# First projection unit among the indexer products, with loads fetched ahead and other homes for five kept units

## The chip, the cores and the metric

The kernel runs on one core of one Trainium2 chip. The metric is the device time of one execution in microseconds. Before the change three runs gave 2064.09, 2066.74 and 2067.27 us; the median is 2066.74 us. Times inside an execution come from one profiled execution, counted from its first instruction.

## The reference, cut to what matters

One layer of a streaming encoder, for 2048 tokens of width 1024, all in float32:

```
xn     = rms_norm(x, norm_gain)
proj   = xn @ w_in          # qa ka va ga | qb kb vb gb | iq ik iw | za zb
ya     = chunked_relpos_attention(qa, ka, va, rel_bias) * silu(ga)
iq, ik = partial_rope(iq), partial_rope(ik)
score  = sum over heads of relu(iq_h . ik) * iw_h      # chunk-causal
idx    = top 256 keys of each query by score
yb     = attention(qb over kb[idx], vb[idx]) * silu(gb)
merged = sigmoid(za + b_a) * (ya @ w_branch_a) + sigmoid(zb + b_b) * (yb @ w_branch_b)
out    = rms_norm(x + merged @ w_out, final_gain)
```

The change touches the projection of x, the loads around it, and where some intermediate results are kept. It changes no product.

## The kernel before, in words

**Precision.** Every float32 product is made from split operands: each operand is a rounded high part and a low part (the rest), and `mm3` (L213) issues three matmuls for each 128-row slice of the contraction: high x high, high x low, low x high. A product over the full width of 1024 and 512 tokens is 8 x 3 = 24 matmuls of 512 columns.

**First phase (L237 to L421), the index projection.** The tokens are four groups of 512. The phase takes them in the order 2, 3, 0, 1, so index i = 0 to 3 stands for groups 2, 3, 0, 1. For each index i there are three products, `chain(i, m)` with m = 0, 1, 2: rotated index queries and keys and part of kb; further index queries; the rest. x of a group lives in one of two slots (groups 2 and 0 in slot 0, groups 3 and 1 in slot 1). For i = 0 and 1 x is used before the norm (`split_u`), and the reciprocal root is multiplied in when the result leaves the accumulator. For i = 2 and 3 it is scaled first (`scaled`, through `split_x`, L231: a VectorE multiply L233, a ScalarE cast L234, a VectorE subtraction L235). The roots come from `squares` (row sums of squares, L287), `root_columns` (VectorE, L297) and `root_rows` (four transposes on TensorE, L307, and a ScalarE copy, L308). The rows of x for the squares are loaded by `load_rows` into tiles of other tags, "xr" and "e" among them. `evac_i` (L321) empties an accumulator: for m = 0 it loads a rotation table "cs" (L328, one buffer) and rotates; then it casts (L340), subtracts (L341) and stores to memory (L347). `weights_t` (L353) transposes the index weights. The seven accumulators of the chains are taken in turn by `rot("first", 7)`: acc0 and acc1 (pool psp), acc2 to acc4 (pool psx), "lg0" and "ptr0" (pool psl).

**Projection units.** The other columns of w_in are 20 units of 256 columns (`UNITS`, L67; unit 0 is the first of zb). `prep(u)` (L192) loads a unit's weights (L207), casts them on ScalarE (L209) and takes the low part on GpSimd (L210), into one of the two "wt" tiles; before the change the first of these uses a staging of two tiles of 128 KB. The two "wt" tiles hold x of index 0 and 2 and the index weights w01 during the first phase. The main loop (L1354) runs a list of jobs; a "std" job is one unit on group 0 or 1, two products of 24 matmuls each (L1373), emptied by `evac` (L688; zb takes a sigmoid with the bias table "bm", L700, and a store, L701). After job 0 the loop prepares unit 1, after job 1 unit 2.

**Half products.** For 18 of the units (`quads`) groups 2 and 3 are made with one product fewer, from sums and differences of x blocks and of weight blocks. A first turn (`first_half`, and `last_half` for the last unit) leaves three partial sums; a last turn (`part`, L1429) adds them in. Partial sums go to memory (`qD`) and come back (`load_sum`), except those of the units in `KEPT`, which stay on chip in tiles lent by `homes` (L1311). `turns` (L1399) sets the order of the last turns. From `last_half` to `part(0, 0)` TensorE's order is written by hand (`held`, a manual schedule). There `combine_pe` (L1247) makes differences of x blocks on TensorE with two unit matrices that `signs` keeps in a tile of tag "xs".

**Logits and search.** Index logits, scores and the threshold search of each block of 128 queries are written as two generators (`logits`, `search`). Every product of the main loop calls `tick`, which lets `pump` (L645) take steps of the two, as many as a budget of 4300 per tick allows by written costs. When both have ended, `search_again` (L578) writes a check: a flag is computed (L585 to L587), VectorE and GpSimd load it (L588) and branch (L589, L590) over a spare arm, `bits_of` (L595), which repeats the search in another way and is normally not run. Attention begins once tick 142 is passed.

**Order.** Except in that hand-written stretch, a planner orders the instructions of each engine at build time, from its own simulated times and the order in the text, with the text's order as priority. All loads and stores in question are issued from SyncE's one queue (SP).

Of the kernel before, what the change touches and what calls it, by code (L numbers as in the profile page):

```python
# [96 lines left out]
def block_kernel(ctx: ExitStack, tc: tile.TileContext, io, dbg=None):  # L97
# [93 lines left out]

    def prep(u, gate=None, at=None):  # L192
        if (at or u) in wcur:
            return
        wt = wpool.tile([128, 2, KT, WT], F32R, name="wt", tag="wt")
        if UNITS[u][0] == "va":
            st = stage[-1][0].tile([128, KT, 32], F32, name="wst", tag="wst", bufs=stage[-1][2])
            nc.sync.dma_start(st, io["wV"][UNITS[u][1]])
            nc.scalar.activation(wt[:, 0, :, 256:288], st, AF.Copy)
            nc.gpsimd.tensor_tensor(wt[:, 1, :, 256:288], st, f32(wt[:, 0, :, 256:288]), op=OP.subtract)  # L200
        for c in range(2):
            pl, n, bufs = stage[-1]
            for k in range(0, KT, n):
                st = pl.tile([128, n, 128], F32, name="wst", tag="wst", bufs=bufs)
                if gate is not None:
                    nc.gpsimd.tensor_copy(st[:, 0, 0:1], gate)
                nc.sync.dma_start(st, io["wP"][u, c, :, k:k + n, :])  # L207
                hi = wt[:, 0, k:k + n, c * 128:(c + 1) * 128]
                nc.scalar.activation(hi, st, AF.Copy)  # L209
                nc.gpsimd.tensor_tensor(wt[:, 1, k:k + n, c * 128:(c + 1) * 128], st, f32(hi), op=OP.subtract)  # L210
        wcur[at or u] = wt
# [19 lines left out]
    def split_x(s, k, src, root):  # L231

        nc.vector.scalar_tensor_tensor(src, src, gcol[:, k:k + 1], root, op0=OP.mult, op1=OP.mult)  # L233
        nc.scalar.activation(xh[s][:, k], src, AF.Copy)  # L234
        nc.vector.tensor_tensor(xl[s][:, k], src, f32(xh[s][:, k]), op=OP.subtract)  # L235

    with ExitStack() as ph:  # L237
# [74 lines left out]
        def chain(i, m, c=all_):  # L312
# [6 lines left out]
            mm3(accs[i, m][:, c], [((w_[0][:, k], w_[1][:, k]), (xh[s_][:, k, c], xl[s_][:, k, c])) for k in range(KT)])  # L319

        def evac_i(i, m):  # L321
            g = order[i]
# [3 lines left out]
            if m == 0:  # L326
                cs = xp.tile([128, 2, 512], F32, name="cs", tag="cs")
                nc.sync.dma_start(cs, io["csI"][:, :, cols])  # L328
                if i < 2:
# [29 lines left out]

        nc.sync.dma_start(gcol, io["g1"])  # L360
        for k in range(0, KT, 2):
            load_x(0, k, k + 2, halves[0])
# [34 lines left out]
        for m in range(3):  # L397
            chain(1, m)
        scaled(2)
        for m in range(3):  # L400
            evac_i(0, m)
        weights_t(0)
        for m in range(3):
            chain(2, m)
        squares(3)
        roots_of(3)
        squares(1)
        roots_of(1)
        scaled(3)
        prep(0)  # L410
        for m in range(3):
            evac_i(1, m)
        weights_t(1)
        for m in range(3):
            evac_i(2, m)
        for m in range(3):
            chain(3, m)
        weights_t(2)
        for m in range(3):
            evac_i(3, m)  # L420
        weights_t(3)  # L421


# [28 lines left out]
    ready, scores, open_ = [], {}, set()  # L452

    iqs = {}

    def load_iq(b):

        iqs[b] = tk.tile([128, H, 128], F32R, name="iqT", tag="iqT", bufs=2)
        for a in range(4):
            nc.sync.dma_start(f32(iqs[b][a * 32:a * 32 + 32]),  # L460
                              iqD[a % 2].rearrange("(d h) n -> d h n", h=H)[:, :, b * 128:b * 128 + 128])

    load_iq(BLOCKS[0])

# [130 lines left out]
    def bits_of(b):  # L595
# [6 lines left out]
        half = sc.bitcast(I16).rearrange("p (n t) -> p n t", t=2)  # L602
        hi, lo, eq = (q.tile([128, S], I16, name="i16" + t, tag=t)[:, :n]
                      for q, t in ((tk, "sc1"), (tkl, "sc2"), (tkl, "sc3")))
        junk = tk.tile([128, S], I16, name="junk16", tag="gt", bufs=2)[:, :n]
# [32 lines left out]

    nc.sync.dma_start(bm, io["bm"])
    threads = {0: logits(), 1: search()}  # L640
# [547 lines left out]
    def tick(x):  # L1188
        due[1] += x
        if threads:  # L1190
            pump(PUMP * x)
# [116 lines left out]

    KEPT, on_chip, free_ = quads[-6:], {}, []

    def homes(n):  # L1311

        while len(free_) < n:
            opened = count_["home"] = count_.get("home", -1) + 1
            if opened < 6:
                assert 0 not in threads
            else:
                assert not threads
            pl, tag, w, bufs = ((xpoolr, "ikT", S, 1), (tk, "iqT", 1024, 2), (tk, "iqT", 1024, 2), (xpoolr, "roots2", 512, 1),
                                (xpoolr, "roots3", 512, 1), (tkl, "xs", 1024, 2),  # L1320
                                (tk, "gt", 1024, 2), (tk, "gt", 1024, 2), (tk, "sc0", SLOTS[0], 1))[opened]
            t = pl.tile([128, w], F32R, name="keep" + tag, tag=tag, bufs=bufs)
# [31 lines left out]
    for i, (how, r_, u, g) in enumerate(jobs):  # L1354
        kind, c2 = UNITS[u]
        wt, s_ = wcur[r_], SLOT[g]
        if how == "one":
            for _ in (last_half if u == quads[-1] else first_half)(u, wt):
                tick(0.5)
        for c in range(0 if how == "one" else 4 if kind == "va" else 2):  # L1360
            acc = next_acc(i)
            if kind == "va":
# [35 lines left out]
    kept_ = list(KEPT)  # L1398
    turns = [(kept_ if q in (0, 1, 3, 5, 7, 9) else plain).pop(0) for q in range(len(quads))]  # L1399

# [210 lines left out]
```

## Time and profile before

| what | us |
| --- | --- |
| median of three runs | 2066.74 |
| profiled execution | 2061.87 |
| its span, first to last instruction | 2060.1 |
| TensorE busy | 1988.3 |
| VectorE busy | 1472.6 |
| ScalarE busy | 1261.9 |
| GpSimd busy | 801.6 |

Engines: PE is TensorE, PEld its weight loads, DVE VectorE, ACT ScalarE, POOL GpSimd, SP SyncE, whose queue issues the transfers. In the timeline a row gives start, length, engine, line, operation, written and read tile, partitions x elements, count; square brackets give the idle time just before it and what ended that. A letter q behind an engine (DVEq) marks work of its sequencer. A matmul's length overlaps the next one's; rates are counts over windows.

### The profile page before, as it was taken

To read this page: it belongs to the slowest core of one execution; us is meant where nothing else is said; L and a number is where in the kernel's file an instruction comes from. 1 tells how busy PE (TensorE), PEld (TensorE's weight loads), DVE (VectorE), ACT (ScalarE), POOL (GpSimd) and SP (SyncE) were. 2 spreads that over 40 slices of the span, in tenths; PEclk is the share of its full clock that TensorE was granted. 3 is DMA by queue.
4 is the path that set the end of the run, shared out by engine and by line. 5 is a ranking of instruction groups with operands and counts; after the bars stand their busy time and mean duration, and the time that the engine had idled before them with its cause. 6 is when DMAs were issued, how large, how long until landed. Compare 5 with 4: busy or idle time off the path is not lost.

```text
span 2060.1 us, 33967 instructions
## 1 busy us (share of the span) xinstructions
PE 1988.3 (97%) x10674; PEld 1690.0 (82%) x10674; DVE 1472.6 (71%) x3646; ACT 1261.9 (61%) x2481; POOL 801.6 (39%) x1045
## 2 busy tenths in 40 slices
PE   8799999999999999999979999999999999999998
PEld 7588888889889888778858889888888888887886
DVE  6749887978789987476446768758886688775534
ACT  5456666556567554247468869858987688773221
POOL 2122233321132464465335464454444633432410
PEclk9899999999999999999979999999999999999999
DMA  9473344374464665378797674564355631325632
GB/s 351 149 241 125 120 139 159 132 208 138 169 196 139 219 219 172 112 235 284 263 275 226 200 231 144 168 222 145 122 155 168 219 103 52 104 88 183 216 136 92
DMA packets 243144, 361.57 MB, mean 176 GB/s; under 512 B 30992, under 2 KB 114320, under 8 KB 242832
## 3 DMA queue, kind: packets, MB, share of 16 engines
q1 hardware_dynamic: 242960, 359.37, 54.3%
q8 instruction: 85, 1.39, 0.3%
q14 instruction: 99, 0.81, 0.1%
HBM read 243.45 MB, written 115.83 MB: 174 GB/s over the span
## 4 chain that ended last, share of the span: by engine, by line
PE 49%; DVE 3%; DMA 3%; ACT 2%; issue 2%; POOL 1%; SPq 0%; DVEq 0%; ACTq 0%; POOLq 0%
PE d L219 9%; PE po L1506 8%; PE acc L219 7%; PE O L1025 6%; PE s L1000 6%; PE pt L1017 5%; PE O L935 3%; PE s L890 3%; PE pt L925 3%; DMA wst<-wS 1%; DVE P L816 1%; DMA kk<-kA 1%; DVE ptl L840 0%; ACT P L1003 0%; DMA kBt<-kB 0%
## 5 line engine op out<-in xcount | busy, mean ns | idle before, releaser
L219 PE MATMUL acc<-xh,wt 128*128 128x512 f32 x2160 | 690.4, 394 | 6.8 <-DVE e L341 2.4
L219 PEld LDWEIGHTS acc<-xh,wt 128*128 128x128 f32 x2160 | 405.1, 188 | 99.1 <-ACT wt L1261 5.0
L219 PE MATMUL acc<-xl,wt 128*128 128x512 f32 x1080 | 423.6, 392 | 0.0
L837 POOL TENSOR_TENSOR ptl<-pf,pth 128x512 fp32r<-128x512 f32 (+1 forms) x144 | 179.9, 1249 | 256.7 <-ACT pf L833 179.5
L219 PEld LDWEIGHTS acc<-xl,wt 128*128 128x128 f32 x1080 | 203.7, 189 | 43.8
L210 POOL TENSOR_TENSOR wt<-wst,wt 128x512 fp32r<-128x512 f32 (+1 forms) x92 | 117.6, 1304 | 269.0 <-ACT wt L209 237.5
L840 DVE TENSOR_TENSOR ptl<-pt,pth 128x512 fp32r<-128x512 f32 (+1 forms) x288 | 187.5, 660 | 45.3 <-ACT pth L839 43.7
L490 DVE SCALAR_TENSOR_TENSOR sc<-lg,iw,sc 128x512 f32<-128x512 f32 (+2 forms) x266 | 178.9, 679 | 42.6 <-ACT lg L485 37.4
L1000 PE MATMUL s<-kBt,qsB 128*128 128x512 f32 (+3 forms) x640 | 187.3, 385 | 2.7 <-DVE mx L816 2.3
L485 ACT ACTIVATE lg<-lg 128x512 f32<-128x512 f32 (+2 forms) x304 | 149.8, 524 | 65.4 <-PE lg L483 63.8
L839 ACT ACTIVATE pth<-pt 128x512 fp32r<-128x512 f32 (+1 forms) x288 | 159.8, 579 | 30.4 <-PE pt L1017 19.9
L1017 PE MATMUL pt<-ident,P 128*128 128x128 f32 x1088 | 166.5, 273 | 1.1 <-DVE ptl L840 0.6
L1003 ACT ACTIVATE P<-P,mx 128x128 f32<-128x128 f32 (+15 forms) x128 | 154.7, 1210 | 18.6 <-DVE mx L816 18.3
L1025 PE MATMUL O<-ptl,vBt 128*128 128x256 f32 x544 | 149.0, 299 | 2.6 <-POOL ptl L837 1.8
L1025 PE MATMUL O<-pth,vBt 128*128 128x256 f32 x544 | 147.6, 289 | 2.5 <-ACT pth L839 1.0
L816 DVE CUSTOM_DVE_ANT_0 P<-s,mk,mx 128x512 f32<-128x512 f32 (+2 forms) x192 | 125.1, 651 | 33.7 <-PE s L1000 27.4
L1017 PEld LDWEIGHTS pt<-ident,P 128*128 128x128 f32 x1088 | 127.5, 140 | 9.2 <-DVE ptl L840 1.8
L890 PE MATMUL s<-kk,qz 128*128 128x320 f32 (+1 forms) x448 | 112.2, 348 | 12.3 <-DMA kk<-kA 8.9
L1064 POOL TENSOR_TENSOR dw<-dst,dw 128x512 fp32r<-128x512 f32 x64 | 83.0, 1298 | 82.3 <-ACT dw L1063 77.9
L1000 PEld LDWEIGHTS s<-kBt,qsB 128*128 128x128 f32 x640 | 102.0, 190 | 15.6 <-DVE mx L816 9.3
L1025 PEld LDWEIGHTS O<-ptl,vBt 128*128 128x128 f32 x544 | 102.6, 189 | 14.0 <-DVE ptl L840 6.7
L1261 ACT ACTIVATE wt<-wst 128x512 fp32r<-128x512 f32 (+1 forms) x144 | 72.9, 567 | 64.1 <-PE acc L219 36.6
(310 smaller groups left out, 4438.2 us busy)
## 6 DMA issues: line engine op xcount, KB each, us to landing
wst<-wP SPq DMA_DIRECT2D x84, 256.0 KB
wst<-wS SPq DMA_DIRECT2D x72, 256.0 KB
kk<-kA SPq DMA_DIRECT2D x56, 256.0 KB
vs<-vA SPq DMA_DIRECT2D x56, 256.0 KB
wst<-wS SPq DMA_DIRECT2D x72, 192.0 KB
qz<-qA SPq DMA_DIRECT2D x96, 128.0 KB
qD<-q SPq DMA_DIRECT2D x36, 256.0 KB
part<-qD SPq DMA_DIRECT2D x36, 256.0 KB
```

What stands on the lines that cost most here:

```text
L219: m = nc.tensor.matmul(acc, a, b, start=(first and i == 0), stop=(last and i == n - 1), **({} if first and last else {"skip_group_check": ...
L485: nc.scalar.activation(lg, lg, AF.Relu)
L490: nc.vector.scalar_tensor_tensor(o_, lg, wv, o_, op0=OP.mult, op1=OP.add)
L837: nc.gpsimd.tensor_tensor(lo, pf, f32(hi), op=OP.subtract)
L839: nc.scalar.activation(hi, src, AF.Copy)
L840: nc.vector.tensor_tensor(lo, src, f32(hi), op=OP.subtract)
L890: nc.tensor.matmul(s_ps[:, :w], q[:, m, j * 128:(j + 1) * 128], kk[:, ko:ko + w], start=(m == 0), stop=(m == 1))
L1000: nc.tensor.matmul(s_ps[:, :w], q[:, h, :], kBt[:, m, a:a + w], start=(m == 0), stop=(m == 1))
L1003: nc.scalar.activation(P[:, e, :n], P[:, e, :n], AF.Exp, bias=mx[:, e:e + 1], scale=-1.0, accum_out=st["sum"][:, (u % 2) * 2 + e:(u % 2) * ...
L1017: nc.tensor.transpose(pt[:, k, e, :], P[:, e, (kt + k) * 128:(kt + k + 1) * 128], ident)
L1025: nc.tensor.matmul(o_, vBt[:, kt + k, :], src[:, k, :], start=(kt + k == 0 and n_ == 0), stop=(kt + k == b and n_ == 1), skip_group_check= ...
L1506: nc.tensor.matmul(accs[t, hf], a, b[:, n_], start=(k == 0 and i == 0), stop=(k == KT - 1 and i == 2))
```

## The change

- Unit 0 on group 0 (job 0 of the main loop) is written in the first phase, after chain(2, ·) and the scaling of index 3. Its accumulators are acc2 and ptr0, and its two results leave with the sigmoid there. The main loop only counts job 0's two ticks.
- Unit 0's weights are prepared after `scaled(2)`, through the six small staging tiles "wis" of the index weights. Unit 1's are prepared the same way before the last `evac_i`.
- chain(2, ·) runs in the order m = 1, 0, 2; chain(2, 1) is emptied early. The root of index 3 is taken before that of index 1 and its transposes stand before chain(2, 2).
- The rotation tables of index 2 and 3 are loaded ahead into "xr" tiles. The first queries of the logits (`load_iq`) are loaded inside the phase. The bias table bm is loaded second, behind the gains.
- For the first four ticks `tick` does not pump.
- Five units are kept on chip instead of six. Their homes are ikT, two iqT, the two roots, sc2 and sc3; the spare arm takes sc1 and the two "xs" tiles. The order of the last turns follows.

```diff
-    def prep(u, gate=None, at=None):
+    def prep(u, gate=None, at=None, via=None):
...
-            pl, n, bufs = stage[-1]
+            pl, n, bufs = via or stage[-1]
             for k in range(0, KT, n):
-                st = pl.tile([128, n, 128], F32, name="wst", tag="wst", bufs=bufs)
+                st = pl.tile([128, n, 128], F32, name="wst", tag="wis" if via else "wst", bufs=bufs)
...
+        turns_ = {}
+
+        def load_cs(i, tag, bufs):
+            cs = xp.tile([128, 2, 512], F32, name="cs", tag=tag, bufs=bufs)
+            nc.sync.dma_start(cs, io["csI"][:, :, order[i] * 512:order[i] * 512 + 512])
+            return cs
...
-                cs = xp.tile([128, 2, 512], F32, name="cs", tag="cs")
-                nc.sync.dma_start(cs, io["csI"][:, :, cols])
+                cs = turns_.pop(i) if i in turns_ else load_cs(i, "cs", 1)
...
         nc.sync.dma_start(gcol, io["g1"])
+        nc.sync.dma_start(bm, io["bm"])
...
         scaled(2)
+        prep(0, via=(xp, 2, 6))
         for m in range(3):
             evac_i(0, m)
         weights_t(0)
-        for m in range(3):
-            chain(2, m)
         squares(3)
-        roots_of(3)
+        root_columns(3, 1)
+        chain(2, 1)
+        chain(2, 0)
+        root_rows(3)
+        chain(2, 2)
+        evac_i(2, 1)
+        scaled(3)
+        for c in range(2):
+            acc = (ps, psl)[c].tile([128, 512], F32, name="xa", tag=("acc2", "ptr0")[c])
+            c_ = slice(c * 128, c * 128 + 128)
+            mm3(acc, [((wcur[0][:, 0, k, c_], wcur[0][:, 1, k, c_]), (xh[0][:, k], xl[0][:, k])) for k in range(KT)])
+            e = ev.tile([128, 512], F32, name="ef", tag="ef")
+            nc.scalar.activation(e, acc, AF.Sigmoid, bias=bm[:, 8 + c:9 + c])
+            nc.sync.dma_start(sBD[0][c_], e)
+        rot("first", 7)
         squares(1)
+        for i in (2, 3):
+            turns_[i] = load_cs(i, "xr", 2)
         roots_of(1)
-        scaled(3)
-        prep(0)
         for m in range(3):
             evac_i(1, m)
         weights_t(1)
-        for m in range(3):
+        for m in (0, 2):
             evac_i(2, m)
         for m in range(3):
             chain(3, m)
         weights_t(2)
+        load_iq(BLOCKS[0])
+        prep(1, via=(xp, 2, 6))
         for m in range(3):
             evac_i(3, m)
...
-        hi, lo, eq = (q.tile([128, S], I16, name="i16" + t, tag=t)[:, :n]
-                      for q, t in ((tk, "sc1"), (tkl, "sc2"), (tkl, "sc3")))
+        hi, lo, eq = (q.tile([128, S], I16, name="i16" + t, tag=t, bufs=n_)[:, :n]
+                      for q, t, n_ in ((tk, "sc1", 1), (tkl, "xs", 2), (tkl, "xs", 2)))
...
-    nc.sync.dma_start(bm, io["bm"])
...
     def tick(x):
         due[1] += x
+        if due[1] <= 4:
+            return
...
-    KEPT, on_chip, free_ = quads[-6:], {}, []
+    KEPT, on_chip, free_ = quads[-5:], {}, []
...
             opened = count_["home"] = count_.get("home", -1) + 1
-            if opened < 6:
-                assert 0 not in threads
-            else:
-                assert not threads
+            assert 0 not in threads and open_ <= set(pairs[-1])
             pl, tag, w, bufs = ((xpoolr, "ikT", S, 1), (tk, "iqT", 1024, 2), (tk, "iqT", 1024, 2), (xpoolr, "roots2", 512, 1),
-                                (xpoolr, "roots3", 512, 1), (tkl, "xs", 1024, 2),
-                                (tk, "gt", 1024, 2), (tk, "gt", 1024, 2), (tk, "sc0", SLOTS[0], 1))[opened]
+                                (xpoolr, "roots3", 512, 1), (tkl, "sc2", SLOTS[2], 1),
+                                (tkl, "sc3", SLOTS[3], 1))[opened]
...
         for c in range(0 if how == "one" else 4 if kind == "va" else 2):
+            if i == 0:
+                tick(1)
+                continue
             acc = next_acc(i)
...
-    turns = [(kept_ if q in (0, 1, 3, 5, 7, 9) else plain).pop(0) for q in range(len(quads))]
+    turns = [(kept_ if q in (0, 1, 3, 5, 7) else plain).pop(0) for q in range(len(quads))]
```

`load_iq` moves up in the text, unchanged, so that the first phase can call it.

More of the change, by code (lines that the diff above doesn't have):

```diff
@@ L235, in split_x, with load_iq @@
         nc.vector.tensor_tensor(xl[s][:, k], src, f32(xh[s][:, k]), op=OP.subtract)
+    iqs = {}
+    def load_iq(b):
+        iqs[b] = tk.tile([128, H, 128], F32R, name="iqT", tag="iqT", bufs=2)
+        for a in range(4):
+            nc.sync.dma_start(f32(iqs[b][a * 32:a * 32 + 32]),
+                              iqD[a % 2].rearrange("(d h) n -> d h n", h=H)[:, :, b * 128:b * 128 + 128])
     with ExitStack() as ph:
@@ L452, in block_kernel @@
     ready, scores, open_ = [], {}, set()
[L454 to L463, printed above, removed]
     def logits():
```

## The prediction

> **What bounds the kernel now.** I read the page first, then the windows table of the opening 125 us, then TensorE's own timeline there, and only then the places that the later edits touch. The page:
>
> ```profile
> span 2060.1 us, 33967 instructions
> PE 1988.3 (97%) x10674; PEld 1690.0 (82%) x10674; DVE 1472.6 (71%) x3646; ACT 1261.9 (61%) x2481; POOL 801.6 (39%) x1045
> PE   8799999999999999999979999999999999999998
> PEclk9899999999999999999979999999999999999999
> ```
>
> TensorE is the bound: 1988.3 of 2060.1 us. An edit that removes no matmul can only win where TensorE stands still or runs below full clock; slices 1, 2 and 21 are such places. The change removes no matmul. The windows table (columns: window, length, busy time and count of each engine, granted clock, DMA share, GB/s), the last three rows of it finer:
>
> ```profile
> 0.00:25.00 25.00, 17.87 (x133) 17.83 (x134) 13.90 (x29) 17.29 (x38) 9.78 (x109) 1.00 0.86 294
> 25.00:50.00 25.00, 23.98 (x112) 19.54 (x112) 15.95 (x42) 12.41 (x25) 0.33 (x1) 1.00 1.03 405
> 50.00:75.00 25.00, 14.72 (x67) 10.93 (x65) 19.09 (x47) 15.37 (x32) 11.00 (x10) 0.89 0.53 179
> 75.00:100.00 25.00, 20.18 (x79) 15.78 (x79) 18.70 (x30) 5.43 (x10) 0.00 (x0) 0.84 0.40 123
> 100.00:125.00 25.00, 24.50 (x103) 19.99 (x104) 4.16 (x7) 8.35 (x16) 1.58 (x2) 0.93 0.82 246
> 77.50:83.20 5.70, 5.26 (x12) 3.80 (x13) 5.64 (x10) 0.00 (x0) 0.00 (x0) 0.50 0.00 0
> 100.50:103.90 3.40, 3.40 (x8) 2.69 (x9) 1.02 (x2) 1.31 (x3) 0.00 (x0) 0.53 0.88 281
> 107.60:119.60 12.00, 12.00 (x53) 9.75 (x52) 0.47 (x1) 2.98 (x5) 0.00 (x0) 1.00 0.82 243
> ```
>
> Between 50 and 100 us TensorE is idle for 10.28 + 4.82 us, and after the pauses it runs at half clock. TensorE's timeline names the pauses:
>
> ```profile
> 52.05 0.62 PE L307 MATMUL trr<-ident,rs10y 128*128 128x128 f32 x4 [1.61 <-DVE rs10y L150]
> 54.08 0.50 PE L219 MATMUL xa<-xh,w 128*128 128x512 f32 x1 [1.41 <-DVE more L338]
> 65.70 0.60 PE L307 MATMUL trr<-ident,rs13y 128*128 128x128 f32 x4
> 68.19 0.65 PE L307 MATMUL trr<-ident,rs11y 128*128 128x128 f32 x4 [1.89 <-ACT work L308]
> 70.05 0.80 PE L219 MATMUL xa<-xh,w 128*128 128x512 f32 x1 [1.20 <-ACT xh L234]
> 77.54 0.80 PE L219 MATMUL xa<-xh,w 128*128 128x512 f32 x1 [6.69 <-DVE more L338]
> 78.74 0.80 PE L219 MATMUL xa<-xl,w 128*128 128x512 f32 x1 [0.40 <-DVE xl L235]
> 100.50 0.79 PE L219 MATMUL acc<-xh,wt 128*128 128x512 f32 x1 [2.38 <-DVE e L341]
> ```
>
> The reader sees one hole: at 65.70 TensorE has run out of index chains and waits until 77.54, because the last group's x (index 3, group 1) must be scaled on VectorE first. The pause at 100.50 is the first unit waiting for two accumulators of chain(2, ·) to be emptied.
>
> **The change, part by part.**
>
> *Unit 0 in the hole.* Its two products on group 0 are 2 x 24 = 48 matmuls of 512 columns. At 12.00/53 = 0.226 us each (row 107.60) they are 10.9 us. They need group 0's x, which chain(2, ·) uses already, and unit 0's weights. The hole from 66.3 (65.70 + 0.60) to 77.54 is 11.2 us wide, so they fit almost exactly. What can go in all: pauses 1.89 + 1.20 + 6.69 + 0.40 + 2.38 = 12.56; half clock, 12 matmuls in 5.26 us where 2.72 would do, 2.5; 8 in 3.40 us for 1.81, 1.6. Together **16.7 us**. The two pauses at 52.05 and 54.08 (3.0 us) I leave: chain(2, 0) and chain(2, 2) still wait for group 2's root to empty their banks.
>
> *What is late next.* Group 3's root transposes (rs11y) now stand behind unit 0, and chain(3, ·) takes the banks of chain(1, ·), which are emptied with that root. The link root, copy, multiply, next matmul showed a pause of 1.41 at 54.08; I charge 1.41 once. What hides the rest is VectorE's lead:
>
> ```profile
> 38.80 5.39 DVE L233 SCALAR_TENSOR_TENSOR xw<-xw,gcol,work 128x512 f32<-128x512 f32 x8 [6.93 <-ACT work L308]
> 68.17 8.59 DVE L233 SCALAR_TENSOR_TENSOR x<-x,gcol,work 128x512 f32<-128x512 f32 x8 [1.27 <-ACT work L308]
> 81.92 3.10 DVE L235 TENSOR_TENSOR xl<-x,xh 128x512 fp32r<-128x512 f32 x5
> 71.92 2.31 POOL L210 TENSOR_TENSOR wt<-wst,wt 128x256 fp32r<-128x256 f32 x2
> 107.76 1.28 ACT L700 ACT_TABLE_LOAD   x1
> 81.95 6.72 SPq L328 DMA_DIRECT2D cs<-csI  x2
> 0.74 0.39 SPq L360 DMA_DIRECT2D gcol<-g  x1
> 40.95 0.33 SPq L639 DMA_DIRECT2D bm<-bm  x1
> ```
>
> Group 1's root is now taken after one chain(2, ·), not two, so its scaling starts some 5 us before 68.17. The same eight instructions took 5.39 us at 38.80 and 8.59 beside GpSimd's subtractions (71.92); six staging tiles instead of two bring those forward to the 50s, so I expect about 5.4, and x ready near 75 to 77 where it was 85.0. If this cover is gone, chain(3, ·) starts no later than before plus a few us, and 10.9 us of products are still behind us.
>
> *Clock after the 1.41.* Here rows differ: after 1.61 + 1.41 us of pauses (52.05, 54.08) the rate held, after 2.38 (100.50) the clock was 0.53. Bounds 0 and 1.6; I take 0.8, the middle. [...]
>
> *Tables ahead, bias table, sigmoid.* The two rotation tables, whose issues held the queue from 81.95 for 6.72 us, come earlier, into tiles that the squares release; the stores behind them come out sooner, so the 2.38 goes. The bias table moves from 40.95, where it hid, to second place in the queue: one issue, 0.33 us there and 0.39 for the like load of gcol at the start, ahead of the first x, and TensorE waits for that. **0.4 us**. The sigmoid's table load (1.28) moves from one place off the path to another; nothing.
>
> *Second unit's weights, first queries.* These are the same loads and casts, earlier. They cover for the fact that only two chains (10.9 us), with no index logits among them, now stand ahead of unit 1. Eight casts and subtractions of 256 columns (first two subtractions 1.42 us at 49.67) are 5.7 us on GpSimd, behind the last use of the index weights; two of the eight tiles need a freed buffer. I take nothing, upper bound in the rivals.
>
> *Four ticks without pumping.* Stepping through the written costs of logits and search (each yields its own; pump spends 4300 a tick) ends both at tick 119 before; the four skipped ticks make it 123, and the units' own ticks end at 124. Search is VectorE work off the path:
>
> ```profile
> L483 PE MATMUL lg<-ikT,iqT x304: 276/393/498, 120.1 to 703.5; 128*128 128x512 f32 x101, 128*128 128x384 f32 x27, 128*128 128x256 f32 x24
> L574 SPq DMA_DIRECT2D mskD<-far x14: 319/326/491, 196.3 to 813.1; - x14
> L1339 ACT ACTIVATE keepgt<-acc x1: 599/599/599, 866.4 to 866.4; 128x512 f32<-128x512 f32 x1
> L588 DVEq TENSOR_LOAD <-flag x1: 542/542/542, 817.3 to 817.3; - x1
> L588 DVEq SEQ_ASSERT  x1: 41/41/41, 822.7 to 822.7; - x1
> 826.82 0.55 POOL L1272 TENSOR_TENSOR wst<-wst 128x128 f32<-128x128 f32 x1 [8.33 <-DMA wst<-wS]
> PE acc L219 <- DVE keepikT L1442: 1.7, 1, 1.7
> PE acc L219 <- ACT wt L1261: 1.0, 1, 1.0
> PE cm L1252 <- DVE keepgt L1304: 0.9, 1, 0.9
> ```
>
> The last mask left at 813.1, 53 us before the last unit's first copy at 866.4, so the search itself can slip. But the branch behind it (L588 to L590) closes VectorE from 817.3 to 822.7, 5.4 us, and today stands where VectorE waits for TensorE anyway. After the change it is written inside last_half, where TensorE's order is fixed by hand, and its spare arm wants both "xs" tiles, one of which holds signs()'s unit matrices. Either puts it at the hand-over around 860 to 890, where TensorE already waits on VectorE and ScalarE (the last three rows, of 855 to 895). Bounds: 0, and 5.4 + 8.33 if VectorE's and GpSimd's stops add; I take **3.5 us**, two thirds of VectorE's stop.
>
> *Five kept units.* One unit more goes by memory: three stores and three loads of 256 KB, against 36 and 36, in a stretch with room:
>
> ```profile
> qD<-q SPq DMA_DIRECT2D x36, 256.0 KB
> 750.00:1000.00 250.00, 244.23 (x1058) 197.81 (x1058) 161.65 (x319) 123.11 (x202) 126.04 (x242) 0.99 0.63 208
> PE s L890 <- DMA kk<-kA: 8.9, 4, 3.4
> ```
>
> At a share of 0.63 they hide; only loads at attention's start, where TensorE waits for them (last row), would cost, and this unit's turn is the tenth of eighteen before that. Nothing.
>
> **Sum.** 16.7 - 1.4 - 0.8 - 0.4 = 14.1 won early, 3.5 lost at the branch: **10.6 us**. The profiled execution took 2061.87 us (span 2060.1 and 1.8 around it), so 2051.3. That execution lies 4.9 below the median 2066.74 of the runs shown; from the median the same sum gives **2056**.
>
> **Rivals.**
>
> *The branch hides again* (the scheduler finds a gap as at 817.3): the 3.5 stays with us, 2066.74 - 14.1 = 2052.6. For it: VectorE is idle between products in last_half; against: the rows of waits there.
>
> *A new wait takes the hole's place*: unit 1's weights. Their loads stand behind the four loads of the first queries, which need the stores of chain(2, ·)'s results; if they start only when chain(3, ·) ends, three late tiles and the 5.7 us chain exceed 10.9 by about 5, and half clock follows (2.5). 10.6 - 7.5 = 3.1, 2063.6, which is no change. For it: the queue is in order and stood 6.72 us at 81.95. Against: six tiles are free by then.
>
> *Slower*: the branch again, but in the worst place: VectorE's 5.4 and GpSimd's 8.33 fall in a row on the weights of the first "last turn" and on A21, both wanted by TensorE at once, and 2.5 of half clock follows: 16.2 against 14.1, so 2069. With an early gain of only 10.9 - 0.4 (x no sooner than before) it is 2072. It decides from a stop of 14 us on.
>
> *The change doesn't do what it says*: unit 0's products run in the hole but push chain(3, ·) by their full 10.9, VectorE being no sooner. Then only the 2.38 and 1.6 go: 4.0 - 0.4 - 3.5, 2066.6. Against: the hole is a wait for VectorE, not for TensorE.
>
> **How the numbers follow.** Forecast 60%, 2056 (own range 2050 to 2061); branch hidden 14%; unit 1's weights 10%; slower 9%; doesn't do what it says 7%. A measurement of this kernel tells about 0.2%, 4.1 us, from no change: faster means below 2062.6. The first two cases lie there and a part of the third: 0.77; no change 0.14; slower 0.09. The range leaves out the worst of the branch at one end and a full 18 us at the other: 2048 to 2067.
>
> **What would show it.** Right: the sigmoid's table load near 70 us instead of 107.76; TensorE's idle time in 50 to 100 us down from 15 to about 5; granted clock there near 1.00; the search's flag read after 840 and TensorE's waits behind it grown by some 3 us. Wrong: a pause over 2 us ahead of chain(3, ·) or of unit 1's first product; first matmul later than 7.6 (25.00 - 17.87 = 7.13 now); attention's start moved by something other than the gains before it.

## The result, and the profile after

The changed kernel took 2051.07 us (median of six runs, 2049.52 to 2051.38). The kernel before took 2065.61 us in the runs beside it (six, 2064.09 to 2067.27). The ratio is 0.9927, with an interval from 0.9917 to 0.9937: 14.5 us won, where 10.6 were forecast, and 2051.07 against a forecast of 2056. The profiled execution of the changed kernel took 2051.24 us.

The page of the kernel after (span and instructions, busy time of each engine, TensorE's busy time and granted clock in 40 slices):

```profile
span 2048.7 us, 34010 instructions
PE 1984.7 (97%) x10674; PEld 1684.9 (82%) x10674; DVE 1468.2 (72%) x3646; ACT 1264.1 (62%) x2486; POOL 792.4 (39%) x1049
PE   8999999999999999999979999999999999999998
PEclk9999999999999999999999999999999999999999
```

No matmul has gone (10674 as before), and the low slices 1 and 2 are now a single one. Where the opening changed, its windows table of the kernel after says (window, length, busy time and count of PE, PEld, DVE, ACT, POOL, then granted clock, DMA share, GB/s; the last row finer):

```profile
25.00:50.00 25.00, 24.79 (x116) 19.83 (x115) 16.44 (x43) 12.58 (x25) 0.86 (x2) 1.00 1.02 393
50.00:75.00 25.00, 20.59 (x84) 16.54 (x85) 17.31 (x47) 14.72 (x31) 7.16 (x8) 0.86 0.83 281
75.00:100.00 25.00, 23.45 (x107) 18.88 (x106) 18.91 (x29) 10.14 (x20) 4.86 (x5) 1.00 0.37 111
100.00:125.00 25.00, 25.00 (x115) 20.60 (x114) 5.04 (x8) 8.36 (x19) 7.69 (x8) 1.00 0.83 236
55.50:60.00 4.50, 4.50 (x11) 3.57 (x12) 3.27 (x6) 2.63 (x6) 2.38 (x2) 0.52 0.65 220
```

TensorE is idle for 4.41 + 1.55 = 5.96 us between 50 and 100 us, where it was 15.10. From 75 to 125 us it runs at full clock, with one pause of 1.55 us. What is left lies between 50 and 60 us: the row of 50 to 75 us counts 84 matmuls against 115 for a full one, and 11 matmuls fill 4.5 us at a clock of 0.52. TensorE's timeline of the kernel after names the pauses that are left, and the start of unit 1:

```profile
53.00 0.65 PE L316 MATMUL trr<-ident,rs10y 128*128 128x128 f32 x2 [3.09 <-DVE rs10y L150]
55.49 0.79 PE L219 MATMUL xa<-xh,w 128*128 128x512 f32 x1 [1.41 <-DVE more L353]
82.83 0.50 PE L219 MATMUL xa<-xh,w 128*128 128x512 f32 x1 [1.55 <-DVE more L353]
100.33 0.48 PE L219 MATMUL acc<-xh,wt 128*128 128x512 f32 x1
```

Totals alone don't say where 14.5 us come from, because the planner wrote a different order on every engine. So the traces are compared by **lead**: each matmul is counted with the usual step from start to start that its shape has in the trace of before (0.230 us for 128x512), and the lead at a place is how much earlier the same sum of matmul work has been issued than in that trace. It is good to about a microsecond, and each trace is one execution, which lies up to 6 us from its kernel's median; places are read from traces, totals from medians.

| lead over before (us), where before stood at | 112 | 183 | 739 | 996 | 1140 | end |
| --- | --- | --- | --- | --- | --- | --- |
| after | 12.9 | 12.9 | 7.7 | 6.2 | 12.9 | 11.8 |
| e1 (early edits alone) | 12.9 | 8.2 | 8.8 | 7.3 | 9.2 | 7.5 |
| e2 (homes and turns alone) | 1.5 | 1.0 | 0.9 | -0.4 | 3.6 | 3.2 |
| e3 (after, no skipped ticks) | 12.6 | 12.4 | 12.1 | 11.5 | 16.6 | 15.9 |
| e4 (after, old last turn) | 12.5 | 12.6 | 8.8 | 8.5 | 8.4 | 7.1 |
| e5 (e2 with skipped ticks) | 2.0 | 1.3 | -1.1 | -1.7 | 3.8 | 3.1 |
| e6 (after, unit 0's loads later) | 20.1 | 18.5 | 14.7 | 15.2 | 22.9 | 21.9 |
| e7 (after, no branch) | 13.6 | 13.0 | 5.6 | 5.2 | 7.9 | 7.0 |
| e8 (after, hole not filled) | 2.9 | 2.4 | -0.6 | -1.7 | 1.7 | 0.5 |
| e9 (e6, no skipped ticks) | 18.6 | 18.4 | 18.0 | 16.1 | 16.8 | 16.6 |
| e10 (after, loads later still) | 13.5 | 11.4 | 8.2 | 7.9 | 8.7 | 8.5 |
| e11 (e6, two skipped ticks) | 17.9 | 17.2 | 14.5 | 8.5 | 12.9 | 12.5 |
| e12 (e2, old last turn) | -0.5 | -0.5 | -1.3 | -2.3 | 1.7 | 0.8 |

In the changed kernel the opening wins 12.9 us; some 7 are lost in the middle, in this trace; and 6.7 come back at 996 to 1140, where attention begins. The forecast knew the first, not the other two. So the questions for the runs were three: is the early gain the filled hole; what are the ticks and the branch worth; and what happens at attention's start, which only the "homes" edit touches.

### The profile page after: what moved, and what is told of

Same layout as the page of the kernel before. It is cut to its first block, busy times and chain, and to the rows that moved or that the text cites. A ratio compares the mean times of both kernels' runs of the same rounds, so it can differ in the third digit from the quotient of the medians.

```text
span 2048.7 us, 34010 instructions
## 1 busy us (share of the span) xinstructions
PE 1984.7 (97%) x10674; PEld 1684.9 (82%) x10674; DVE 1468.2 (72%) x3646; ACT 1264.1 (62%) x2486; POOL 792.4 (39%) x1049
## 4 chain that ended last, share of the span: by engine, by line
PE 45%; DMA 3%; DVE 3%; ACT 2%; issue 2%; POOL 1%; SPq 0%; DVEq 0%; POOLq 0%; ACTq 0%
PE d L219 8%; PE acc L219 7%; PE po L1526 6%; PE O L1043 6%; PE s L1018 5%; PE pt L1035 5%; PE O L953 3%; PE pt L943 2%; PE s L908 2%; DMA mf<-mD 1%; DVE P L834 1%; DMA vs<-vA 1%; DMA sg<-gAD 1%; DVE ptl L858 0%; ACT P L1021 0%
## 5 line engine op out<-in xcount | busy, mean ns | idle before, releaser
L219 PE MATMUL acc<-xh,wt 128*128 128x512 f32 x2128 | 680.4, 393 | 5.2 <-ACT wt L1281 2.5
L219 PEld LDWEIGHTS acc<-xh,wt 128*128 128x128 f32 x2128 | 398.3, 188 | 97.0 <-ACT wt L1281 3.8
L219 PE MATMUL acc<-xl,wt 128*128 128x512 f32 x1064 | 416.6, 392 | 0.1
L1043 PEld LDWEIGHTS O<-pth,vBt 128*128 128x128 f32 x544 | 102.8, 189 | 10.3 <-ACT pth L857 4.0
```

The costliest lines, as they stand in the source:

```text
L219: m = nc.tensor.matmul(acc, a, b, start=(first and i == 0), stop=(last and i == n - 1), **({} if first and last else {"skip_group_check": ...
L1043: nc.tensor.matmul(o_, vBt[:, kt + k, :], src[:, k, :], start=(kt + k == 0 and n_ == 0), stop=(kt + k == b and n_ == 1), skip_group_check= ...
```

## The experiments

Each ratio stands beside runs of the kernel before on the same chip.

| run | median us | ratio to before | interval |
| --- | --- | --- | --- |
| after | 2051.07 | 0.9927 | 0.9917 to 0.9937 |
| e1 early edits alone | 2053.99 | 0.9939 | 0.9926 to 0.9951 |
| e2 homes and turns alone | 2058.99 | 0.9970 | 0.9959 to 0.9981 |
| e3 after, no skipped ticks | 2049.26 | 0.9926 | 0.9913 to 0.9938 |
| e5 e2 with skipped ticks | 2063.77 | 0.9990 | 0.9981 to 0.9999 |
| e4 after, old last turn | 2057.24 | 0.9958 | 0.9942 to 0.9974 |
| e6 after, unit 0's loads later | 2042.52 | 0.9893 | 0.9879 to 0.9908 |
| e7 after, no branch | 2049.28 | 0.9917 | 0.9904 to 0.9929 |
| e8 after, hole not filled | 2062.25 | 0.9989 | 0.9980 to 0.9997 |
| e9 e6, no skipped ticks | 2042.62 | 0.9893 | 0.9877 to 0.9910 |
| e10 after, loads later still | 2056.75 | 0.9962 | 0.9949 to 0.9975 |
| e11 e6, two skipped ticks | 2048.72 | 0.9926 | 0.9912 to 0.9940 |
| e12 e2, old last turn | 2064.75 | 1.0008 | 0.9995 to 1.0021 |

### The parts apart: e1, e2, e3, e5

**e1** keeps the early edits and takes back the skipped ticks and the homes:

```diff
-        if due[1] <= 4:
-            return
-    KEPT, on_chip, free_ = quads[-5:], {}, []
+    KEPT, on_chip, free_ = quads[-6:], {}, []
...
-    turns = [(kept_ if q in (0, 1, 3, 5, 7) else plain).pop(0) for q in range(len(quads))]
+    turns = [(kept_ if q in (0, 1, 3, 5, 7, 9) else plain).pop(0) for q in range(len(quads))]
```

with the old list of homes and the old tiles of the spare arm.

> The changed kernel with its first-phase edits only: unit 0 in the hole, loads ahead, bias table early. The four skipped ticks, the five kept units, their homes and the order of the last turns are as before. Theory A (read off the two traces: first phase wins 12.9 us, the four ticks lose 7 in the middle, the homes and turn order win 6.7 at attention's start, the branch costs nothing): 2065.6 - 12.9 = 2053, with a lead of about 13 us at 130 us that stays flat to the end. Theory B (the losses and gains after 300 us come from the planner's re-ordering after any shift, not from those edits): the lead changes by several us somewhere between 300 and 1100 us all the same, total anywhere from 2046 to 2060. Theory C (the prediction's sum): 2065.6 - 14.1 = 2051.5.

**e2** is the reverse, the kernel before with the new homes, spare arm tiles, five kept units and turns, and nothing else:

```diff
-    KEPT, on_chip, free_ = quads[-6:], {}, []
+    KEPT, on_chip, free_ = quads[-5:], {}, []
...
-    turns = [(kept_ if q in (0, 1, 3, 5, 7, 9) else plain).pop(0) for q in range(len(quads))]
+    turns = [(kept_ if q in (0, 1, 3, 5, 7) else plain).pop(0) for q in range(len(quads))]
```

> The kernel before with only the late edits: five kept units, their new homes, the spare arm's tiles and the order of the last turns. No edit of the first phase, no skipped ticks. Theory A: 2065.6 - 6.7 = 2059, all of it at attention's start (first loads of attention issued some 13 us ahead of the last unit product instead of 3), nothing before 1000 us. Theory B: within 3 us of 2065.6, without that pattern. Theory C: 2065.6.

**e3** is the kernel after without the skipped ticks:

```diff
         due[1] += x
-        if due[1] <= 4:
-            return
```

> The changed kernel with pumping from the first tick on, so logits and search are written four ticks earlier; all else as changed. Theory A: the 7 us lost between 300 and 800 us come back, 2051.1 - 7 = 2044. Theory B: 2051 give or take 4, the loss stays or moves. Theory C: the search ends before the last unit, the branch hides, 2051.1 - 3.5 = 2047.6.

**e5** is e2 with the skipped ticks:

```diff
         due[1] += x
+        if due[1] <= 4:
+            return
```

> The kernel before with the late edits and the four skipped ticks, without any edit of the first phase. Theory A: + 7 - 6.7, about 2066. Theory B: no forecast, but the loss between 300 and 800 us need not be there. Theory C: 2065.6 + 3.5 = 2069, lost at the branch between 860 and 890 us.

The early edits alone win 11.0 us (2064.97 beside 2053.99), the homes and turns alone 6.0, and together, without the skipped ticks, 15.7 (e3): nearly the sum. So the edit behind "five kept units", which the prediction priced at nothing, is worth about 6 us; which part of it, e4 and e12 below ask.

The skipped ticks give no clear answer in the totals. In e5 they cost 4.8 (2063.77 against 2058.99); in e3, taken out of the kernel after, they change the ratio by nothing (0.9926 and 0.9927). In the traces they show in one kind of wait: index logits that wait for the accumulator, because the scores of the logits before have not been taken yet. TensorE's waits between 250 and 850 us (line waited for: us in total, times, longest) of after:

```profile
PE lg L502 <- DVE sc L509: 5.2, 5, 1.9
```

and of e3:

```profile
PE lg L502 <- DVE sc L509: 1.3, 1, 1.3
```

The same wait is 1.6 us in before and 3.1 in e5. All traces follow this: 1.3 to 1.6 us in the six that skip no tick, 3.1 to 5.7 in the seven that skip four, 2.3 in e11, which skips two.

### Branch and hole: e7, e8

**e7** leaves out the repeated search and the branch to it; the flag is still computed:

```diff
-        v = {e: nc.values_load(flag[0:1, 0:1], engines=[e], min_val=0, max_val=1)
-             for e in (mybir.EngineType.DVE, mybir.EngineType.Pool)}
-        for arm in tc.Switch(v, 2):
-            if arm == 1:
-                for b in BLOCKS:
-                    bits_of(b)
```

> The changed kernel without the branch and its spare arm (the flag is still computed, nothing loads it; this leaves out the repeated search, which does not run on these inputs). The prediction's term: 2051.1 - 3.5 = 2047.6. By the traces (lead 6.8 ahead of it, 6.2 behind it): 2050.5.

2049.28 us, ratio 0.9917 against 0.9927: by the medians the branch costs about 2 us, and by the intervals, which overlap, perhaps nothing. It did move where the prediction said. Of the kernel after, the flag's load (duration in ns, start in us), VectorE's stop behind the branch, and TensorE's waits between 882 and 892 us:

```profile
L607 DVEq TENSOR_LOAD <-flag x1: 542/542/542, 865.3 to 865.3; - x1
```

```profile
881.13 0.86 DVE L1282 TENSOR_TENSOR wt<-wst,wt 128x384 fp32r<-128x384 f32 x1
885.37 0.56 DVE L1282 TENSOR_TENSOR wt<-wst,wt 128x384 fp32r<-128x384 f32 x1 [3.38 <-issue]
```

```profile
PE acc L219 <- DVE wt L1282: 0.2, 1, 0.2
```

VectorE stands for 3.38 us, close to the 3.5 that were charged, but TensorE waits 0.2 us at that place. The lead falls by 0.4 us in the 40 us of work around it.

**e8** leaves job 0 in the main loop and does nothing in the hole; unit 0's weights still come early:

```diff
-        for c in range(2):
-            acc = (ps, psl)[c].tile([128, 512], F32, name="xa", tag=("acc2", "ptr0")[c])
-            ...
-        rot("first", 7)
...
-            if i == 0:
-                tick(1)
-                continue
```

> The changed kernel, but unit 0's two products on group 0 stand in the main loop again; loads, tables, order of the index chains and all late edits as changed. If the products in the hole are the gain: the lead at 130 us falls from 12.9 to about 2 or 3 (the pause at 100 us alone goes) and the total to about 2061. If the loads ahead and the new order of roots had closed the hole by themselves: the lead stays over 8, total about 2054.

2062.25 us, ratio 0.9989: of 14.5 us some 3 are left, and that is about what e5 keeps (0.9990), which has none of the early edits. Without the filling all the others together move the total by little. TensorE's timeline of e8 has the hole again:

```profile
78.48 0.80 PE L219 MATMUL xa<-xh,w 128*128 128x512 f32 x1 [5.77 <-DVE more L353]
```

and its window after it the slow clock:

```profile
75.00:100.00 25.00, 21.12 (x83) 16.76 (x84) 20.46 (x33) 8.72 (x19) 3.09 (x5) 0.81 0.34 98
```

The lead at 112 us is 2.9 instead of 12.9. The early gain is the hole's filling, not the tables or the earlier loads.

### What grew at 53 us: e6, e9, e10, e11

In the kernel after, the pause before the transposes of group 2's root (rs10y, L316) is 3.09 us where before it was 1.61. The timeline of VectorE and of GpSimd in the kernel after shows why:

```profile
49.12 0.16 DVE L150 SCALAR_TENSOR_TENSOR rs10y<-rs10a,rs10y 128x4 f32<-128x4 f32 x1
...
49.95 0.65 DVE L149 TENSOR_TENSOR rs10a<-rs10a,v 128x4 f32<-128x4 f32 x1
50.64 0.65 DVE L150 SCALAR_TENSOR_TENSOR rs10y<-rs10a,rs10y 128x4 f32<-128x4 f32 x1
```

```profile
49.14 3.50 POOL L210 TENSOR_TENSOR wt<-wst,wt 128x256 fp32r<-128x256 f32 x5 [28.30 <-ACT wt L209]
```

A root's steps of 128x4 take 0.16 us until 49.14, when GpSimd begins to subtract unit 0's weights, and 0.60 to 0.65 beside it. GpSimd's instructions take 3.50 / 5 = 0.70 each, and five of VectorE's steps in a row, from 49.31 to 52.65, take nearly as long. In before two such subtractions (1.42 us from 49.67) already stood beside this root, and two of its steps were long (0.59 and 0.65); here there are five of each.

**e6** makes unit 0's loads wait for a root, so that the subtractions fall behind the root steps:

```diff
-        prep(0, via=(xp, 2, 6))
+        prep(0, gate=roots_[0][:, 0:1], via=(xp, 2, 6))
```

> The changed kernel, with unit 0's weight loads held back until group 2's root is there (a GpSimd copy of one column of it into each staging tile), so that GpSimd's eight subtractions do not run beside VectorE's short root steps at 49 to 53 us. Theory: TensorE's pause ahead of the root transposes grew from 1.61 to 3.09 us by that contention and 2 us of half clock followed; it goes back to about 1.6 without half clock, lead at 130 us 15 to 16 instead of 12.9, total 2048. Rival 1: the pause has another cause and stays. Rival 2: the weights are now late for the hole, the lead at 130 us falls under 11.

The gate in this text was misnamed: `roots_[0]` is group 0's root (index 2), whose transposes begin at 36.43 us in e6's trace, 13.6 us ahead of group 2's; the text recorded for e9 puts that right. e6 took 2042.52 us (2040.68 to 2046.94), ratio 0.9893: it beats the kernel after by about 7 us (0.9927 - 0.9893, of 2065). VectorE, GpSimd and TensorE of e6 at the same place, and its windows:

```profile
48.75 0.16 DVE L148 TENSOR_TENSOR rs10a<-rs10y 128x4 f32<-128x4 f32 x1
48.95 0.16 DVE L149 TENSOR_TENSOR rs10a<-rs10a,v 128x4 f32<-128x4 f32 x1
```

```profile
55.84 1.45 POOL L210 TENSOR_TENSOR wt<-wst,wt 128x256 fp32r<-128x256 f32 x2 [2.07 <-DMA wst<-wP]
```

```profile
50.04 0.62 PE L316 MATMUL trr<-ident,rs10y 128*128 128x128 f32 x4 [0.56 <-DVE rs10y L150]
52.08 0.50 PE L219 MATMUL xa<-xh,w 128*128 128x512 f32 x1 [1.41 <-DVE more L353]
```

```profile
50.00:75.00 25.00, 23.55 (x110) 19.19 (x111) 22.04 (x48) 17.96 (x36) 11.27 (x12) 1.00 0.83 274
75.00:100.00 25.00, 25.00 (x116) 20.37 (x115) 18.30 (x26) 7.39 (x18) 7.77 (x8) 1.00 0.49 141
```

The steps are short again: with no subtraction beside them the first pause is 0.56, where it was 1.61 with two and 3.09 with five. No slow clock follows in this trace (1.00 in both windows), and the pause of 1.55 ahead of chain(3, ·) is gone as well: between 75 and 100 us TensorE doesn't stop. (The planner now puts group 3's root transposes at 69.68 us, inside unit 0's products; in after they stand behind them, at 80.67.) 2.5 + about 2 of slow clock + 1.55 make 6.1 of the 7.2 us by which the lead at 112 us grew (20.1 against 12.9); the last microsecond isn't placed. The gate is worth the same in a second base: e9, below, against e3, neither with skipped ticks, is 0.9893 against 0.9926. The missing slow clock may be luck: behind pauses of 1.60 and 1.41 us the clock is 0.50 in e2, behind 1.61 and 1.41 it is 1.00 in before (last section).

**e10** uses group 2's root itself, the one whose steps are in question, as the gate:

```diff
-        prep(0, via=(xp, 2, 6))
+        prep(0, gate=roots_[2][:, 0:1], via=(xp, 2, 6))
```

> The changed kernel with unit 0's weight loads gated by group 2's root, the one whose steps were slowed. Theory: the short root steps take 0.16 us throughout and the pause ahead of the transposes is under 1, as with the earlier gate; the weights come later (casts from about 55 us), still in time for the products at 63 to 66; total 2042 to 2045. Rival: weights late, a pause of 2 to 5 us ahead of unit 0's products, 2046 to 2050.

2056.75 us, ratio 0.9962, slower than the kernel after. The pause ahead of group 2's transposes is short here too, 0.69 us, and unit 0's products begin at 63.94 without a pause, so the weights are not late. The wait has gone to chain(3, ·), 3.21 us, with slow clock behind it (0.86 between 75 and 100 us): VectorE empties chain(1, ·) (L353) at 78.58, right behind the subtractions of index 3's x. TensorE's timeline of e10, and its window:

```profile
79.32 0.79 PE L219 MATMUL xa<-xh,w 128*128 128x512 f32 x1 [3.21 <-DVE more L353]
```

```profile
75.00:100.00 25.00, 21.79 (x89) 17.44 (x89) 17.22 (x27) 7.78 (x18) 8.61 (x7) 0.86 0.46 134
```

By the lead at 112 us, 13.5, this opening is no worse than that of after, 12.9. The 5.7 us in the medians are lost behind it: the lead falls to 11.4 by 183 us, and attention's start gains 0.8 where that of after gains 6.7. Why was not found. Of the three places tried for unit 0's loads, e6's gives by far the best opening.

**e9** is e6 without the skipped ticks, **e11** is e6 with two instead of four:

```diff
-        if due[1] <= 4:
-            return
```

> The run with gated weight loads (whose gate was group 0's root, taken at 38 us, not group 2's as its expectation said), and pumping from the first tick on. Theory: the four skipped ticks cost some 3 to 5 us between 300 and 800 us by pushing logits and search later, also here; lead ahead of attention 18 to 19 instead of 15, total 2042.5 - 4 = 2038.5. Rival: the early trace of the run with only the first-phase edits showed that early pumping can cost as much at 130 us (a logits product in TensorE's order waiting for scores); then 2042 to 2043, the loss only moved.

```diff
-        if due[1] <= 4:
+        if due[1] <= 2:
             return
```

> Gated weight loads (group 0's root) and two skipped ticks instead of four, the two of job 0, which has no products in the main loop any more. Theory: half of the loss by the four ticks, 2040.5. Rival: as with none or four, within 1 of either.

e9 took 2042.62 us, the same as e6; e11 took 2048.72, 6 us more than either. No theory of a cost per skipped tick gives 0, 6 and 0 for zero, two and four of them. The logits' wait for the scores does follow the ticks (1.3 us in e9, 2.3 in e11, 4.1 in e6), and between 112 and 739 us e9 loses 0.6 us of lead and e6 5.4; but at attention's start e9 gains 0.7 and e6 7.7. What e11 loses shows in TensorE's waits between 700 and 850 us:

```profile
PE acc L219 <- DVE q L1324: 3.2, 3, 2.5
PE acc L219 <- DVE el L737: 2.1, 1, 2.1
```

waits which neither before nor e6 has there; e11's lead falls from 14.5 at 739 us to 8.7 at 850. They come from the planner's other order; what in it decides was not found.

### The last turn: e4, e12

`plain` takes the places in `turns` that kept units leave. With one kept unit less, a unit of gb goes to the end of `plain` and so has the very last turn, where before a unit of ka had it. **e4** is the kernel after with that unit put at the tenth place, ka again last; **e12** is e2 with the same line:

```diff
     plain = [u for u in quads if u not in KEPT]
+    plain.insert(4, plain.pop())
     kept_ = list(KEPT)
```

> The changed kernel, but the unit that lost its home takes its last turn at the tenth place, where a kept unit stood before, so that the units after it follow in the old order and ka is the last again instead of gb. If attention's earlier start comes from the order of the last turns (gb's end leaves one store per product, ka's two casts and two stores, and attention's first loads stand behind them in the one queue): 2051 + 6 = 2057. If it comes from the homes and the tiles that they free: 2051, as the changed kernel.

> The kernel before with five kept units and the new homes, but the last turns in the old order of kinds, ka last. With gb last the same kernel took 2059.0. If the order of the last turns is the gain at attention's start: 2065, as the kernel before, with attention's first loads issued some 3 us ahead of the last unit product. If the homes or the number of kept units are: 2059.

e4 took 2057.24 us (ratio 0.9958), 6 us more than the kernel after. e12 took 2064.75 us (ratio 1.0008), 6 more than e2 and the same as the kernel before. The intervals of each pair don't touch. So new homes, five kept units and new tiles for the spare arm are worth nothing, and the order of the last turns is worth all of it. The line moves every turn from the tenth on by one; that the very last one decides is read from the queue below, not shown by a run of its own.

A part of it shows in SP's queue and in one wait. The queue of before, of after and of e4, around the first loads of attention (qz, kk):

```profile
1029.87 0.32 SPq L724 DMA_DIRECT2D kA<-part  x1
1030.40 1.78 SPq L851 DMA_DIRECT2D qz<-qA  x3
```

```profile
1014.01 0.32 SPq L742 DMA_DIRECT2D kA<-part  x1
1015.17 0.32 SPq L1444 DMA_DIRECT2D part<-qD  x1
1015.71 1.78 SPq L869 DMA_DIRECT2D qz<-qA  x3
```

```profile
1024.45 0.33 SPq L742 DMA_DIRECT2D kA<-part  x1
1025.00 1.80 SPq L869 DMA_DIRECT2D qz<-qA  x3
```

In each the first load stands behind the last store of ka, in after with one load of a partial sum between them. The last matmul of the units ends at 1033.2, 1028.7 and 1032.0: the load leaves 2.8 us ahead of that in before, 13.0 in after and 7.0 in e4 (13.1 in e2, 7.0 in e12). Then TensorE waits less for the keys. Its waits for them between 950 and 1100 us are 8.9 us in before (the row that the prediction shows); after's and e4's are:

```profile
PE s L908 <- DMA kk<-kA: 3.5, 2, 2.1
```

```profile
PE s L908 <- DMA kk<-kA: 6.0, 2, 3.9
```

With ka last this wait is 8.9, 5.6 (e1), 6.0 and 5.1 (e12); with gb last it is 3.5, 2.4 (e2), 2.2 (e3), 2.7 (e5), 3.1 (e6), 3.1 (e7), 2.3 (e8), 3.5 (e9), 5.3 (e10) and 2.7 (e11). The means, 6.4 and 3.1, are 3.3 us apart, and the two ranges overlap a little. That is about half of the 6 us. The rest is not placed: the traces' leads between 996 and 1140 us go from a gain of 0.7 (e9) to one of 7.7 (e6) with gb last, and e2, with gb last, gains the same 4.0 there as e12 with ka last. So the totals show that the order is worth 6 us, twice; by which way is shown in part.

## Why the prediction was right, and where it was not

**Right**, and shown: unit 0's products fit the hole (e8), and the pauses and the slow clock from 66 us on went. Of the forecast's 14.1 us at the opening 12.9 came. Most of the named signs came too: the sigmoid's table is loaded at 74.96 us (near 70 was said), idle time between 50 and 100 us is 5.96 us (about 5), the flag is read at 865.3 (after 840). The granted clock, said to be near 1.00, is so only from 75 us on and 0.86 between 50 and 75. Index 3's x is scaled in 5.39 us, as said; the pause ahead of chain(3, ·) is 1.55 us, where 1.4 was charged. The rows of VectorE and ScalarE in the kernel after:

```profile
71.54 5.39 DVE L233 SCALAR_TENSOR_TENSOR x<-x,gcol,work 128x512 f32<-128x512 f32 x8 [2.85 <-ACT work L317]
76.84 4.90 DVE L235 TENSOR_TENSOR xl<-x,xh 128x512 fp32r<-128x512 f32 x8
```

```profile
74.96 1.28 ACT L433 ACT_TABLE_LOAD   x1
```

The rival of unit 1's weights fell: unit 1 starts at 100.33 with no pause before it. The rival that the hole is not filled fell, and so did the slower one. Bias table: TensorE's busy time in the first 25 us is the old one within 0.1, and the lead at 20 us of work is 0.35 us behind (0.3 to 0.9 in e1, e3, e6 and e7); 0.4 was charged.

**Step that failed: "The two pauses at 52.05 and 54.08 (3.0 us) I leave".** They became 3.09 + 1.41 = 4.5 us, with 11 matmuls at half clock behind (0.52, 55.50 to 60.00), some 2 us: 3.4 us lost, and at 50 us of work the trace of after is 3.4 us behind that of before. The prediction saw that GpSimd's subtractions come forward "to the 50s" and counted it as a relief for VectorE's scaling; it did not ask whom they meet there. e6, which keeps them off the root, is 7 us faster.

**Step that failed: "its scaling starts some 5 us before 68.17".** It starts at 71.54, and x is ready at 81.74 (76.84 + 4.90), where 75 to 77 was said. VectorE has group 1's root at 63.11, but the root's transposes stand on TensorE behind two products of chain(2, ·), not one, and behind the losses at 53 us:

```profile
70.27 0.60 PE L316 MATMUL trr<-ident,rs13y 128*128 128x128 f32 x4
```

Before, they stood at 65.70. It seems to have cost little: unit 0's products covered it, and the wait of 1.55 us ahead of chain(3, ·) is put down to its accumulators (L353) and not to x.

**Step that was mis-sized: the clock term of 0.8.** After the 1.55 us pause ahead of chain(3, ·) the clock is 1.00 (window 75 to 100), and so it is in e1, e3 and e4, where TensorE is idle in that window for 1.55, 1.55 and 1.56 us; the term is 0 there. The slow clock (0.52) came where nothing was charged, at 55.5 us.

**Step that failed: the branch, 3.5 us.** VectorE's stop moved as described and lasted 3.38 us, but TensorE waited 0.2 us there, and e7 gained 2 by the medians, if anything: the step from VectorE's stop to TensorE's, argued from the waits of 855 to 895, does not hold. The rival "the branch hides again" was the true one in its price, though the branch hid at the hand-over itself and not in a gap elsewhere.

**Step that failed: "Five kept units ... Nothing", because "this unit's turn is the tenth of eighteen".** It is the eighteenth; the tenth place went to another unit. The 6 us of the last turns hang on that. e4 is the kernel as the prediction had read it, with the tenth place, and took 2057.24 us, 8.1 below the kernel before beside it. The prediction itself named "attention's start moved by something other than the gains before it" as a sign of being wrong, and that is what happened.

**Step that was left out: the skipped ticks' logits.** The prediction followed the search, which has room, and not the index logits, whose waits for the scores grew from 1.6 to 5.2 us. In the totals this appears in e5 (4.8) and not in e3 against after, nor in e9 against e6, so it is given back elsewhere by a way that stays open.

By places the trace of after reads 12.9 - 6.7 (middle, branch included) + 6.7 - 1.1 (to the end) = 11.8 us, and the median 14.5, against 14.1 - 3.5 = 10.6. The forecast's own range, 2050 to 2061, held the time because the gain it didn't see (6) and the loss it didn't need to charge (3.5) outweighed the losses it had not seen, not because each term was right. To that extent the number is luck; so is it that the profiled execution took 2051.24 us, where the prediction's sum from the profiled execution of before gives 2051.3.

## What to carry to other kernels

Fill a hole with work whose operands are ready, and then look at what the preparation of that work meets where it now runs: here the moved GpSimd subtractions cost some 7 us, more than half of what the filled opening had won, until they were held back by a dependence on an earlier root (e6, 2042.52 us). When a list is shortened, write out the order that follows from it: which units come last can decide how early the next phase's first loads can leave. Where a planner rearranges everything, check a small edit by its exact opposite in a second base, as e4 and e12 do; e3, e5, e9 and e11 show how an edit can be worth 0, 5 and 6 us at once.

## What was not expected of the hardware

**Short VectorE steps beside GpSimd.** In after the root's 128x4 steps (L148 to L150) take 0.16 us alone and 0.60 to 0.65 us beside GpSimd's 128x256 subtractions of 0.70 us, about four times as long. The root is a chain of such steps with TensorE waiting at its end, so it cost a pause of 3.09 us instead of 0.56 (e6).

**The granted clock after a pause.** The length of a pause doesn't settle whether the clock is slow behind it. It stayed full (1.00) after 1.55 us (after, 82.80 to 86.20), 0.56 + 1.41 (e6, 50 to 75), 1.61 + 1.41 (before, 53.40 to 56.80) and 2.82 (e2). It was slow after 1.60 + 1.41 (e2, 0.50), 2.38 (before, 0.53), 3.09 + 1.41 (after, 0.52), 3.21 (e10, 0.86 over 25 us), 5.77 (e8, 0.81 over 25 us), and 2.74 in e1 (0.73), whose pause and window after it (TensorE's timeline, windows) are:

```profile
133.68 0.39 PE L502 MATMUL lg<-ikT,iqT 128*128 128x256 f32 x1 [2.74 <-DVE sc L509]
```

```profile
133.60:140.00 6.40, 6.33 (x22) 5.24 (x23) 5.55 (x11) 2.69 (x6) 0.00 (x0) 0.73 0.83 230
```

That one costs e1 most of the 4.7 us of lead it loses between 112 and 183. The plainest pairs are the opening of e2, the same as that of before and yet slow, and the first product of a unit in e2, which waits longer than in before (2.82 against 2.38) and runs at full clock (1.00 against 0.53). Two pauses of e2 and the windows behind them:

```profile
53.96 0.50 PE L219 MATMUL xa<-xh,w 128*128 128x512 f32 x1 [1.41 <-DVE more L338]
100.44 0.50 PE L219 MATMUL acc<-xh,wt 128*128 128x512 f32 x1 [2.82 <-DVE e L341]
```

```profile
54.50:57.90 3.40, 3.40 (x9) 2.66 (x8) 2.17 (x6) 2.83 (x6) 1.14 (x1) 0.50 0.08 29
100.40:103.80 3.40, 3.37 (x15) 2.76 (x16) 1.00 (x2) 1.32 (x3) 0.00 (x0) 1.00 0.87 292
```

In the clock records of before and after each slow stretch (0.50) between the start and the last 10 us lasts 3.4, 6.8, 10.2 or 13.7 us: in before 13.7 from 69.6 us, 3.4 from 100.3, 878.5 and 1052.6, and 10.2 from 1035.5 and 1073.1; in after 6.8 from 53.0, and 3.4 from 606.0, 1036.1 and 1042.9. What sets these lengths, and which pause is followed by one, no run here shows. So, by the pairs above, a term like the prediction's 0.8, between 0 and 1.6, is as much as can be said of one such pause ahead of time.
